# A two-layer trunk on one core: the feed forwards' norm moved into x, and twelve more column pairs by seven products

## The chip, the cores and the metric

The kernel runs on one core of a Trainium2 chip. The metric is the device time of one execution in microseconds (us); the median of several executions is compared. Engines are named as in the profile: PE (TensorE), DVE (VectorE), ACT (ScalarE), POOL (GpSimd) and SP (SyncE, which only issues DMAs).

## The reference

The input is one sequence of 512 tokens with 1024 channels. Everything is float32. Two layers run one after the other; every layer is a half-step feed forward, a mixing block and a second half-step feed forward.

```
def rms_norm(x, g):  return x * rsqrt(mean(x*x, -1) + 1e-6) * g
def swiglu(h, w_in, w_out):               # w_in 1024 x 5632, w_out 2816 x 1024
    gate, up = split(h @ w_in, 2, axis=-1)
    return (silu(gate) * up) @ w_out

layer 0:  x = x + 0.5 * swiglu(rms_norm(x, g), w_in, w_out)      # FFN1
          x = x + rwkv7_time_mix(rms_norm(x, mix_norm))          # a scan over 512 tokens, in chunks
          x = x + 0.5 * swiglu(rms_norm(x, g), w_in, w_out)      # FFN2
          k, v = shared_kv(x)                                    # keys and values, once
layer 1:  x = x + 0.5 * swiglu(rms_norm(x, g), w_in, w_out)      # FFN3
          x = x + diff_attention(rms_norm(x, mix_norm), k, v)
          x = x + 0.5 * swiglu(rms_norm(x, g), w_in, w_out)      # FFN4
```

## The kernel before

x stays on the chip as eight tiles of 128 channels by 512 tokens. A float32 product is three matmuls in fp32r (mm3, L200 to L202): each operand is split into a rounded part `hi` and the rest `lo`, and hi·hi, hi·lo and lo·hi are added in PSUM. A weight block comes by DMA into `wraw` (two buffers), ACT casts it into `whi` (L146), DVE subtracts it into `wlo` (L147); there are three buffers of each.

The stages follow each other in the trace: FFN1 (0 to 367 us), the time mix (367 to 790, with a scan over chunks from about 580 to 748), FFN2 (790 to 1147), keys and values (1147 to 1241.5), FFN3 (1241.5 to 1600.6), attention (1600.6 to 1776), FFN4 (1776 to the end).

A feed forward works on 22 blocks of 128 gate and 128 up columns, in eleven pairs j = 0, 2, ..., 20. Before it starts, x times the norm's gain g is split into `xgh` and `xgl` (eight tiles each, ten buffers). The factor that the norm still lacks is R, 1/rms of every token: the sum of squares goes through a matmul with ones (L272), ACT takes the root (L367 to L369) and DVE refines it (L370, L371). R is multiplied in after the products, since it is one number per token: `finish` computes g = pg·R (L399, DVE), silu (L400, ACT), u = pu·R (L401, DVE), u·g (L402, POOL) and splits the result into `act` for the product with w_out. The order of the work is pairs 0 to 8, the product with w_out over blocks 0 to 7, pairs 10 to 16, the next product with w_out, pairs 18 and 20, the last one.

A pair has one of two forms. The regular form is 96 matmuls of 512 tokens: 2 blocks, gate and up, 8 channel tiles, 3 matmuls. The form called `quads` takes the 2x2 blocks of a pair (gate and up columns by two halves of the channels, tokens in halves) and uses seven products in place of eight, by Strassen's scheme as Winograd arranged it: 7 x 2 x 4 x 3 = 168 matmuls of 256 tokens. It needs sums of weight blocks (made on DVE in `tmp` and in `wraw` itself, L464 to L473) and sums of halves of x (token_sums, L408 to L428, once for each feed forward, in the tile `tc`, in FFN1 in `BK`). A quad holds both `wraw` buffers and one `tmp` tile, and its products go to g and u by additions, with R multiplied in at L475, L477 and L480. The argument `seven` lists the pairs in this form: (4, 8, 10, 14) in FFN1, (4, 8, 10, 14, 18) in FFN2 and FFN4, none in FFN3, where keys and values hold the room that the sums of x would need. That is 14 quads.

Which instruction follows which on an engine is not the order of the code: a scheduler with a model of its own writes it out when the kernel is built. On the chip every engine then works through its list in that order, so an instruction that waits holds back everything behind it on its engine. SP's list holds the DMA issues.

In the scan, the argument LEAD is the number of steps by which the preparation of a unit (a chunk and a group of heads) runs ahead of its use.

Of the kernel before, what the change touches and what calls it, by code (L numbers as in the profile page):

```python
# [25 lines left out]
class Net:  # L26
# [358 lines left out]
    def ffn(self, xs, goff, w_in, w_out, aside=iter(()), xg=None, pgs=None, new_norm=True, dst=None, seven=(), sums_at=None):  # L385
# [4 lines left out]
        with tc.tile_pool(name=self.name("ffn"), bufs=2) as pool:  # L390
# [19 lines left out]
            def token_sums():  # L410


                hl = self.tl(*(sums_at or (pool, "tc")), (P, 4, 2, 4, H), F32R, bufs=1)
                for k in range(4):
                    g = [self.v("ffn_norm", goff + k + 4 * i) for i in range(2)]
                    y = self.tl(self.gp, "nsq", bufs=2)
                    nc.scalar.activation(y, xs[k], AF.Copy, scale=g[0])
# [1 line left out]
                    for i, x, gx, z in (
                        (0, xs[k][:, half[1]], g[0], y[:, half[0]]),  # L420
                        (1, xs[k + 4][:, half[1]], g[1], t[:, 0]),
                        (2, xs[k + 4][:, half[1]], g[1], y[:, half[1]]),
                        (3, xs[k + 4][:, half[0]], g[1], t[:, 1]),
                    ):
                        nc.vector.scalar_tensor_tensor(t[:, i], x, gx, z, ALU.mult, ALU.subtract)
# [1089 lines left out]
```

## Time and profile before

| | us |
|---|---|
| median of 3 runs | 2117.89 (2116.23 to 2120.51) |
| the profiled execution, own time | 2121.1 |
| its span | 2119.4 |
| PE busy in it | 2083.5 (98%) |
| DVE busy | 1382.8 (65%) |
| ACT busy | 884.5 (42%) |
| POOL busy | 184.2 (9%) |

The profile is of one execution, whose own time is 3.2 us above the median of the runs; 1.7 us of it lie outside the span. TensorE's mean granted clock in it was 0.996 of full speed. A timeline row gives the start of an instruction, its duration, engine, line, operation and operands, and in brackets how long the engine stood idle before it and on what. A duration is from start to end, and the ends of matmuls overlap the starts of the next, so the pace of matmuls is read from their starts. Likewise DVE and ACT begin the next instruction a little before the last has ended: two dependent instructions take their full durations, independent ones follow some 0.09 us sooner.

### The profile page before, as it was taken

What the parts mean: (1) busy time and instruction counts of PE and PEld (TensorE: products, weight loads), DVE (VectorE), ACT (ScalarE), POOL (GpSimd) and SP (SyncE); (2) the same over time, 40 slices, a digit from 0 to 9 for tenths busy, and PEclk for the clock granted to TensorE, in tenths of its full rate; (3) what the DMA queues carried; (4) which work ended last, traced back from release to release, by engine and by line L of the source; (5) the groups of instructions that cost most, each with busy time, mean ns of one, the idle gap of its engine ahead of it and who ended that gap; (6) DMA issues with size and microseconds to landing.
All of it is one profiled execution on the core that took longest, in us unless ns stands there. A gap on an engine that the chain in (4) does not pass through costs nothing.

```text
span 2119.4 us, 28879 instructions
## 1 busy us (share of the span) xinstructions
PE 2083.5 (98%) x11471; PEld 1798.4 (85%) x11471; DVE 1382.8 (65%) x2126; ACT 884.5 (42%) x1459; POOL 184.2 (9%) x226
## 2 busy tenths in 40 slices
PE   9999999999989999999999999999999999999999
PEld 7889888778889978989888988888889778989887
DVE  7857745897977767757466445445356857857563
ACT  6423324687235545323234343223235855423332
POOL 1100001000222201000000001001010210100000
PEclk9999999999999999999999999999999999999999
DMA  5232423336655542323323233333322112232332
GB/s 161 80 120 80 139 95 117 111 135 159 159 138 119 125 132 67 120 80 120 101 92 107 82 98 99 100 100 100 99 80 80 41 47 93 80 120 80 120 100 79
DMA packets 273139, 220.07 MB, mean 104 GB/s; under 512 B 85738, under 2 KB 257932, under 8 KB 273004
## 3 DMA queue, kind: packets, MB, share of 16 engines
q1 hardware_dynamic: 273004, 218.22, 33.8%
q8 instruction: 90, 1.47, 0.3%
q14 instruction: 45, 0.37, 0.1%
HBM read 193.55 MB, written 16.25 MB: 99 GB/s over the span
## 4 chain that ended last, share of the span: by engine, by line
PE 85%; DVE 8%; ACT 3%; DMA 3%; issue 1%; SPq 0%; POOL 0%; DVEq 0%; ACTq 0%; POOLq 0%
PE ps L200 26%; PE ps L201 26%; PE ps L202 25%; ACT s L1304 1%; PE ps L1082 1%; PE ps L1108 1%; DVE wlo L147 1%; PE ps L898 1%; PE ps L1064 1%; DMA g_d<-t 1%; PE ps L1070 1%; PE ps L1099 1%; PE ps L1097 0%; ACT whi L146 0%; DVE t L808 0%
## 5 line engine op out<-in xcount | busy, mean ns | idle before, releaser
L200 PE MATMUL ps<-xgh,whi 128*128 128x512 f32 (+1 forms) x1560 | 573.4, 369 | 1.5 <-ACT whi L146 1.0
L201 PE MATMUL ps<-xgl,whi 128*128 128x512 f32 (+1 forms) x1560 | 572.8, 367 | 0.5 <-DVE xgl L208 0.5
L202 PE MATMUL ps<-xgh,wlo 128*128 128x512 f32 (+1 forms) x1560 | 568.9, 368 | 0.4 <-DVE wlo L147 0.3
L146 ACT CAST whi<-wraw 128x1024 fp32r<-128x1024 f32 (+2 forms) x240 | 243.1, 1023 | 589.0 <-PE ps L201 447.7
L147 DVE TENSOR_TENSOR wlo<-wraw,whi 128x1024 fp32r<-128x1024 f32 (+2 forms) x240 | 311.9, 1303 | 59.3 <-ACT whi L146 53.5
L200 PEld LDWEIGHTS ps<-xgh,whi 128*128 128x128 f32 x1560 | 294.8, 189 | 53.0 <-ACT whi L146 3.2
L202 PEld LDWEIGHTS ps<-xgh,wlo 128*128 128x128 f32 x1560 | 294.5, 189 | 49.9 <-DVE wlo L147 1.4
L201 PEld LDWEIGHTS ps<-xgl,whi 128*128 128x128 f32 x1560 | 294.9, 189 | 49.2 <-issue 1.0
L201 PE MATMUL ps<-actl,whi 128*128 128x512 f32 x656 | 255.3, 389 | 0.0
L200 PE MATMUL ps<-acth,whi 128*128 128x512 f32 x656 | 254.9, 389 | 0.0
L202 PE MATMUL ps<-acth,wlo 128*128 128x512 f32 x656 | 254.3, 389 | 0.0
L402 POOL TENSOR_TENSOR u<-u,g 128x512 f32<-128x512 f32 x60 | 96.6, 1613 | 1409.0 <-DVE u L401 880.9
L528 DVE SCALAR_TENSOR_TENSOR x<-ps,x 128x512 f32<-128x512 f32 x88 | 60.5, 690 | 187.4 <-PE ps L202 187.4
L202 PEld LDWEIGHTS ps<-acth,wlo 128*128 128x128 f32 x656 | 123.1, 188 | 25.6
L200 PEld LDWEIGHTS ps<-acth,whi 128*128 128x128 f32 x656 | 123.1, 188 | 25.6
L201 PEld LDWEIGHTS ps<-actl,whi 128*128 128x128 f32 x656 | 123.1, 188 | 25.4
L447 ACT CAST whi<-wraw 128x1024 fp32r<-128x1024 f32 x70 | 73.5, 1050 | 130.9 <-PE ps L201 121.5
L200 PE MATMUL ps<-whi,xgh 128*128 128x256 f32 (+1 forms) x384 | 123.3, 323 | 0.2 <-DVE mx L1299 0.2
L401 DVE TENSOR_TENSOR u<-ps,R 128x512 f32<-128x512 f32 x60 | 41.3, 688 | 125.5 <-PE ps L202 125.5
L201 PE MATMUL ps<-wlo,xgh 128*128 128x256 f32 (+1 forms) x384 | 122.5, 319 | 0.6 <-DVE wlo L182 0.6
L202 PE MATMUL ps<-whi,xgl 128*128 128x256 f32 (+1 forms) x384 | 122.2, 318 | 0.0
L448 DVE TENSOR_TENSOR wlo<-wraw,whi 128x1024 fp32r<-128x1024 f32 x70 | 94.3, 1347 | 17.7 <-ACT whi L447 17.1
(393 smaller groups left out, 3268.1 us busy)
## 6 DMA issues: line engine op xcount, KB each, us to landing
wraw<-in_ffn_w_in_dram SPq DMA_DIRECT2D x87, 1024.0 KB
wraw<-in_ffn_w_out_dram SPq DMA_DIRECT2D x34, 1024.0 KB
wraw<-in_rwkv_w_rkv_dram SPq DMA_DIRECT2D x12, 1024.0 KB
wraw<-in_ffn_w_out_dram SPq DMA_DIRECT2D x12, 768.0 KB
wraw<-in_w_kv_dram SPq DMA_DIRECT2D x8, 1024.0 KB
am_d<-nsq SPq DMA_DIRECT2D x16, 256.0 KB
AM<-am_d SPq DMA_DIRECT2D x16, 256.0 KB
wraw<-in_diff_w_q_dram SPq DMA_DIRECT2D x4, 1024.0 KB
```

Source lines behind the costliest of these rows:

```text
L146: self.nc.scalar.copy(hi[:, ks], raw[:, :, c : c + P])
L147: (eng or self.nc.vector).tensor_sub(lo[:, ks], raw[:, :, c : c + P], hi[:, ks].bitcast(F32))
L200: mm(ps, wh, xh, start=start, stop=False)
L201: mm(ps, wh, xl, start=False, stop=False)
L202: mm(ps, wl, xh, start=False, stop=stop)
L401: nc.vector.tensor_mul(u, pu, self.R)
L402: nc.gpsimd.tensor_mul(u, u, g)
L447: nc.scalar.copy(hi, w)
L448: nc.vector.tensor_sub(lo, w, hi.bitcast(F32))
L528: nc.vector.scalar_tensor_tensor(x, ps, 0.5, x, ALU.mult, ALU.add)
L898: mm(ps[:, c, :], abd[:, c0 + c, :], BK[:, p, c0 + c, :], start=True, stop=True)
L1064: mm(pw[:, p, 0:L], Mo[:, p, :], DT[:, p, :].rearrange("p (h t) -> p h t", h=2)[:, :, 32:], start=True, stop=True)
```

## The change

For the blocks of pair 0 all stays as it was, but that u·g is now on DVE. After pair 0's products a new function `normed` computes y = x·g·R for the eight tiles (L422), splits y into new `xgh` and `xgl` (L207, L208) and makes the sums of halves from y by plain subtractions (L429 to L434). From pair 2 on the products come out with the norm in them: `finish` takes silu straight from PSUM (L405) and multiplies (L406), and the quads lose their three multiplications by R.

The lists `seven` grow to (6, 8, 10, 12, 14) in FFN1 and (6, 8, 10, 12, 14, 16, 18) in FFN2, FFN3 and FFN4: 26 quads. Now quads follow one another without a regular pair between them: 6 and 8, then 10, 12, 14 and (but for FFN1) 16. For FFN3 to have room for its sums, keys and values go out to DRAM before it (four DMAs of 1 MB issued by POOL) and come back before attention (four by SP). LEAD goes from 4 to 5.

```diff
             def finish(j, pg, pu):
                 if j % 2 == 0:
                     gu[:] = [self.tl(pool, n, (P, 2, T), bufs=1) for n in ("g", "u")]
                 g, u = (t[:, j % 2] for t in gu)
-                nc.vector.tensor_mul(g, pg, self.R)
-                nc.scalar.activation(g, g, AF.Silu)
-                nc.vector.tensor_mul(u, pu, self.R)
-                nc.gpsimd.tensor_mul(u, u, g)
+                if j < 2:
+                    nc.vector.tensor_mul(g, pg, self.R)
+                    nc.scalar.activation(g, g, AF.Silu)
+                    nc.vector.tensor_mul(u, pu, self.R)
+                    nc.vector.tensor_mul(u, u, g)
+                else:
+                    nc.scalar.activation(g, pg, AF.Silu)
+                    nc.vector.tensor_mul(u, pu, g)
                 acts[j] = self.split(pool, u, "act", 12)
...
-            def token_sums():
+            def normed():
                 hl = self.tl(*(sums_at or (pool, "tc")), (P, 4, 2, 4, H), F32R, bufs=1)
+                ys, new = {}, {}
+                for k in range(KT):
+                    y = ys[k] = self.tl(pool, "actl" if k // 4 else "acth", bufs=12)
+                    nc.vector.scalar_tensor_tensor(y, xs[k], self.v("ffn_norm", goff + k), self.R, ALU.mult, ALU.mult)
+                    new[k] = self.split(self.gp, y, "xg", XB)
+                xg[:] = [new[k] for k in range(KT)]
                 for k in range(4):
...
+                    b = [[ys[k + 4 * i][:, half[c]] for c in range(2)] for i in range(2)]
+                    sub = nc.vector.tensor_sub
+                    sub(t[:, 0], b[0][1], b[0][0])
...
                     nc.scalar.copy(hl[:, k, 0], t)
...
             def quads(j):
-                mul(g, g, self.R.unsqueeze(1).to_broadcast([P, 2, T]))
                 nc.scalar.activation(g, g, AF.Silu)
-                mul(c22, c22, R[1])
                 mul(c22, c22, c12)
                 add(c21, c21, prod(split(a22), tsum(3)))
-                mul(c21, c21, R[0])
                 mul(c21, c21, c11)
...
                     if new_norm:
                         self.R = self.rstd(xs, NORM_EPS)
-                    if seven:
-                        token_sums()
+                    normed()
                     for c in (0, 1):
                         finish(c, pg[c], pu[c])
...
-        NCH, L, G, LEAD = 8, 64, 4, 4
+        NCH, L, G, LEAD = 8, 64, 4, 5
...
-    net.ffn(xs, 0, w_in, ffn_w_out[0, 0], prepare(), xg, pgs, seven=(4, 8, 10, 14), sums_at=(net.bkp, "BK"))
+    net.ffn(xs, 0, w_in, ffn_w_out[0, 0], prepare(), xg, pgs, seven=(6, 8, 10, 12, 14), sums_at=(net.bkp, "BK"))
...
-    net.ffn(xs, KT, ffn_w_in[0, 1], ffn_w_out[0, 1], seven=(4, 8, 10, 14, 18))
+    net.ffn(xs, KT, ffn_w_in[0, 1], ffn_w_out[0, 1], seven=(6, 8, 10, 12, 14, 16, 18))
...
         net.shared_kv(xs, w_kv, kT, vN, gk)
-        net.ffn(xs, 2 * KT, ffn_w_in[1, 0], ffn_w_out[1, 0], new_norm=False)
+        for t, t_d in zip(flat, (kd, vd)):
+            for h in range(2):
+                tc.nc.gpsimd.dma_start(t_d[:, h], t[:, h])
+    net.ffn(xs, 2 * KT, ffn_w_in[1, 0], ffn_w_out[1, 0], new_norm=False, seven=(6, 8, 10, 12, 14, 16, 18))
+        kT, vN, flat = keys_values(kvq)
+        for t, t_d in zip(flat, (kd, vd)):
+            for h in range(2):
+                tc.nc.sync.dma_start(t[:, h], t_d[:, h])
         net.attention(
...
-    net.ffn(xs, 3 * KT, ffn_w_in[1, 1], ffn_w_out[1, 1], dst=out[0], seven=(4, 8, 10, 14, 18))
+    net.ffn(xs, 3 * KT, ffn_w_in[1, 1], ffn_w_out[1, 1], dst=out[0], seven=(6, 8, 10, 12, 14, 16, 18))
```

How the lists of the engines change is shown at three places. Numbers behind a name tell its buffers apart; `ps` is a PSUM tile.

PE at the end of FFN2's pair 0, before the change. ps_7060 and ps_7061 are pair 0's last two results, xgh and xgl are x·g; L272 is the matmul with ones that R hangs on.

```order
L201 MATMUL ps_7061<-xgl_7007,whi_7054 128x512
L200 MATMUL ps_7060<-xgh_7034,whi_7050 128x512
L201 MATMUL ps_7060<-xgl_7035,whi_7050 128x512
L202 MATMUL ps_7060<-xgh_7034,wlo_7051 128x512
L272 MATMUL ps_7181<-nacc_7158,ones 128x512
L202 MATMUL ps_7061<-xgh_7006,wlo_7055 128x512
L200 MATMUL ps_7061<-xgh_7010,whi_7054 128x512
```

22 more matmuls of pair 0 stand behind L272, and the next pair's behind them without a new operand.

The same place in the change. ps_7164 is the last result of pair 0; ps_7409, ps_7410 and ps_7467 belong to pair 2; xgh_7297 and xgl_7298 are the first tile of the new x·g·R.

```order
L202 MATMUL ps_7164<-xgh_7133,wlo_7158 128x512
L200 MATMUL ps_7164<-xgh_7137,whi_7157 128x512
L201 MATMUL ps_7164<-xgl_7138,whi_7157 128x512
L202 MATMUL ps_7164<-xgh_7137,wlo_7158 128x512
L272 MATMUL ps_7284<-nacc_7261,ones 128x512
L200 MATMUL ps_7409<-xgh_7297,whi_7391 128x512
L200 MATMUL ps_7410<-xgh_7297,whi_7401 128x512
L200 MATMUL ps_7467<-xgh_7297,whi_7395 128x512
L201 MATMUL ps_7409<-xgl_7298,whi_7391 128x512
L202 MATMUL ps_7409<-xgh_7297,wlo_7392 128x512
```

L272 has moved behind the last product of pair 0, and right behind it stand products of pair 2 that read the new tiles.

DVE at that place, before: L370 and L371 finish R; L399 and L401 are pair 0's multiplications by R; wlo_7259 is of a later weight block.

```order
L370 TENSOR_TENSOR nr_t_7185<-nr_t_7185,nr_a_7184 128x512
L425 SCALAR_TENSOR_TENSOR tmp_7221<-x_1022_6753,vec_103,tmp_7221 128x256
L371 SCALAR_TENSOR_TENSOR R_7183<-nr_t_7185,R_7183 128x512
L425 SCALAR_TENSOR_TENSOR tmp_7221<-x_1022_6753,vec_103,tmp_7221 128x256
L399 TENSOR_TENSOR g_7228<-ps_7058,R_7183 128x512
L401 TENSOR_TENSOR u_7229<-ps_7060,R_7183 128x512
L399 TENSOR_TENSOR g_7228<-ps_7059,R_7183 128x512
L401 TENSOR_TENSOR u_7229<-ps_7061,R_7183 128x512
L147 TENSOR_TENSOR wlo_7259<-wraw_7256,whi_7258 128x1024
L427 TENSOR_TENSOR tc_7191<-tmp_7221,tc_7191 128x1024
```

Nothing here makes an operand of pair 2's first products.

DVE at that place in the change: L422 makes y, in tiles that go by the names acth and actl; L400 and L402 are pair 0's multiplications by R; L429 is the first of the sums; L208 makes the new xgl.

```order
L422 SCALAR_TENSOR_TENSOR actl_7319<-x_1051_6855,vec_103,R_7286 128x512
L422 SCALAR_TENSOR_TENSOR actl_7325<-x_1051_6855,vec_103,R_7286 128x512
L422 SCALAR_TENSOR_TENSOR actl_7331<-x_1052_6856,vec_103,R_7286 128x512
L422 SCALAR_TENSOR_TENSOR actl_7337<-x_1052_6856,vec_103,R_7286 128x512
L400 TENSOR_TENSOR g_7371<-ps_7161,R_7286 128x512
L402 TENSOR_TENSOR u_7372<-ps_7163,R_7286 128x512
L400 TENSOR_TENSOR g_7371<-ps_7162,R_7286 128x512
L402 TENSOR_TENSOR u_7372<-ps_7164,R_7286 128x512
L429 TENSOR_TENSOR tmp_7343<-acth_7295 128x256
L208 TENSOR_TENSOR xgl_7298<-acth_7295,xgh_7297 128x512
L208 TENSOR_TENSOR xgl_7304<-acth_7301,xgh_7303 128x512
L208 TENSOR_TENSOR xgl_7310<-acth_7307,xgh_7309 128x512
```

Between R and the first xgl that pair 2 reads stand eight L422, four multiplications and a subtraction.

DVE at the end of FFN2's quad 10, before, where a regular pair follows: L448 and L469 to L480 belong to the quad; L147 are the next pair's weights.

```order
L448 TENSOR_TENSOR wlo_8439<-wraw_8243,whi_8438 128x1024
L471 TENSOR_TENSOR u_8248<-u_8248,ps_8376 128x2x256
L472 TENSOR_TENSOR u_8248<-u_8248,ps_8284 128x2x256
L477 TENSOR_TENSOR u_8248<-u_8248,R_7183 128x2x256
L147 TENSOR_TENSOR wlo_8481<-wraw_8478,whi_8480 128x1024
L474 TENSOR_TENSOR g_8247<-g_8247,ps_8408 128x2x256
L147 TENSOR_TENSOR wlo_8485<-wraw_8478,whi_8484 128x1024
L475 TENSOR_TENSOR g_8247<-g_8247,R_7183 128x1024
L479 TENSOR_TENSOR u_8248<-u_8248,ps_8442 128x2x256
L147 TENSOR_TENSOR wlo_8491<-wraw_8488,whi_8490 128x1024
L480 TENSOR_TENSOR u_8248<-u_8248,R_7183 128x2x256
L478 TENSOR_TENSOR u_8248<-u_8248,g_8247 128x2x256
```

The regular pair's weights are split among the quad's last additions and multiplications.

DVE at the end of FFN2's quad 10 in the change, where quad 12 follows: u_8377 and g_8376 belong to quad 10, L470 is quad 12's first sum of weights, and the L454 are its first two splits; L483 adds the last product of quad 10.

```order
L478 TENSOR_TENSOR u_8377<-u_8377,ps_8413 128x2x256
L454 TENSOR_TENSOR wlo_8612<-wraw_8604,whi_8611 128x1024
L480 TENSOR_TENSOR g_8376<-g_8376,ps_8537 128x2x256
L470 TENSOR_TENSOR tmp_8608<-wraw_8605 128x1024
L483 TENSOR_TENSOR u_8377<-u_8377,ps_8569 128x2x256
L482 TENSOR_TENSOR u_8377<-u_8377,g_8376 128x2x256
L476 TENSOR_TENSOR wraw_8605<-wraw_8604,wraw_8605 128x1024
L484 TENSOR_TENSOR u_8377<-u_8377,g_8376 128x2x256
L454 TENSOR_TENSOR wlo_8643<-tmp_8608,whi_8642 128x1024
L208 TENSOR_TENSOR actl_8597<-u_8377,acth_8596 128x512
```

Quad 12's second split (wlo_8643) now stands behind L483, which needs quad 10's last product, and behind three more.

## Rows read from the trace of the kernel before

**Rows 1.** The page: busy time by engine; the chain that ended last, by engine.

```profile
PE 2083.5 (98%) x11471; PEld 1798.4 (85%) x11471; DVE 1382.8 (65%) x2126; ACT 884.5 (42%) x1459; POOL 184.2 (9%) x226
...
PE 85%; DVE 8%; ACT 3%; DMA 3%; issue 1%; SPq 0%; POOL 0%; DVEq 0%; ACTq 0%; POOLq 0%
```

**Rows 2.** Windows: stretch, its us, busy of each engine, PEclk, DMA share, GB/s.

```profile
859.19:880.98 21.79, 21.79 (x98) 18.03 (x97) 17.69 (x20) 8.01 (x10) 2.11 (x1) 1.00 0.30 97
944.68:964.83 20.15, 20.15 (x169) 20.14 (x168) 14.47 (x16) 7.74 (x8) 0.00 (x0) 1.00 0.34 106
56.06:77.69 21.63, 21.03 (x170) 20.39 (x169) 18.28 (x21) 9.10 (x10) 2.14 (x1) 1.00 0.31 98
1803.96:1824.61 20.65, 20.41 (x169) 20.20 (x168) 17.56 (x20) 8.79 (x10) 1.29 (x1) 1.00 0.31 101
```

**Rows 3.** PE's timeline where FFN2's pair 2 goes over into quad 4.

```profile
880.75 0.39 PE L202 MATMUL ps<-xgh,wlo 128*128 128x512 f32 x1
880.98 0.28 PE L200 MATMUL ps<-xgh,whi 128*128 128x256 f32 x1
881.10 0.28 PE L201 MATMUL ps<-xgl,whi 128*128 128x256 f32 x1
```

**Rows 4.** PE's timeline in the scan, at two waits.

```profile
615.84 0.49 PE L1129 MATMUL ps<-xgl,bd 128*128 128x512 f32 x1
620.78 1.38 PE L1064 MATMUL ps<-whi,wlo 128*128 128x64 f32 x8 [4.44 <-DMA whi<-inv_d]
...
726.98 1.25 PE L1108 MATMUL ps<-KM,Vb 128*128 128x128 f32 x5 [1.24 <-DVE KM L1101]
```

**Rows 5.** Windows behind those two waits, columns as in rows 2.

```profile
622.00:624.00 2.00, 2.00 (x11) 2.00 (x11) 1.74 (x6) 0.30 (x1) 0.93 (x3) 0.50 0.09 12
...
727.00:731.00 4.00, 4.00 (x20) 3.79 (x21) 2.84 (x10) 2.62 (x9) 1.49 (x4) 0.57 0.91 220
```

**Rows 6.** Timelines of PE, ACT and DVE where FFN2's R is made.

```profile
811.39 1.02 PE L272 MATMUL ps<-nacc,ones 128*128 128x512 f32 x2
...
813.26 0.68 ACT L367 ACTIVATE R<-ps,bias 128x512 f32<-128x512 f32 x1
...
814.41 0.62 ACT L369 ACTIVATE nr_t<-R 128x512 f32<-128x512 f32 x1
...
818.22 0.68 DVE L401 TENSOR_TENSOR u<-ps,R 128x512 f32<-128x512 f32 x1
818.82 0.68 DVE L399 TENSOR_TENSOR g<-ps,R 128x512 f32<-128x512 f32 x1
```

**Rows 7.** The instructions of line 727, x·g·R in the time mix (duration in ns).

```profile
L727 DVE SCALAR_TENSOR_TENSOR h<-x,vec,R x8: 742/744/746, 383.7 to 388.4; 128x512 f32<-128x512 f32 x8
```

**Rows 8.** ACT's timeline before FFN1's R, and at the end of keys and values.

```profile
29.96 1.28 ACT L367 ACT_TABLE_LOAD   x1
...
1239.71 2.73 ACT L1229 ACTIVATE vN<-ps,Rn 128x512 f32<-128x512 f32 x4 [1.96 <-PE ps L202]
```

**Rows 9.** Timelines of SP and ACT at the end of FFN2's quad 10; a DMA issue; attention.

```profile
956.09 2.95 SPq L135 DMA_DIRECT2D wraw<-in_ffn_w_in_dram  x2
...
961.35 2.00 ACT L146 CAST whi<-wraw 128x1024 fp32r<-128x1024 f32 x2 [3.97 <-DMA wraw<-in_ffn_w_in_dram]
...
1631.62 1.13 PE L1298 MATMUL ps<-kT,qT 64*128 64x512 f32 x4
```

**Rows 10.** DVE's timeline at the end of FFN2's quad 10.

```profile
963.57 0.68 DVE L474 TENSOR_TENSOR g<-g,ps 128x512 f32<-128x512 f32 x1
...
965.31 1.22 DVE L475 TENSOR_TENSOR g<-g,R 128x1024 f32<-128x1024 f32 x1
966.44 0.68 DVE L479 TENSOR_TENSOR u<-u,ps 128x512 f32<-128x512 f32 x1
```

**Rows 11.** ACT's cast of a weight block in quads, by line.

```profile
L447 ACT CAST whi<-wraw 128x1024 fp32r<-128x1024 f32 x70 | 73.5, 1050 | 130.9 <-PE ps L201 121.5
```

**Rows 12.** The chain, a DMA that writes 256 KB to DRAM.

```profile
415.21 6.25 DMA g_d<-t
```

More of the change, by code (lines that the diff above doesn't have):

```diff
@@ L408, in ffn @@
             half = (slice(0, H), slice(H, T))
-            def token_sums():
+            def normed():
                 hl = self.tl(*(sums_at or (pool, "tc")), (P, 4, 2, 4, H), F32R, bufs=1)
+                ys, new = {}, {}
[4 more added lines that the diff above has]
+                xg[:] = [new[k] for k in range(KT)]
                 for k in range(4):
-                    g = [self.v("ffn_norm", goff + k + 4 * i) for i in range(2)]
-                    y = self.tl(self.gp, "nsq", bufs=2)
-                    nc.scalar.activation(y, xs[k], AF.Copy, scale=g[0])
+                    b = [[ys[k + 4 * i][:, half[c]] for c in range(2)] for i in range(2)]
                     t = self.tl(pool, "tmp", (P, 4, H), bufs=1)
[L419 to L425, printed above, removed]
+                    sub = nc.vector.tensor_sub
+                    sub(t[:, 0], b[0][1], b[0][0])
+                    sub(t[:, 1], b[1][1], t[:, 0])
+                    sub(t[:, 2], b[1][1], b[0][1])
+                    sub(t[:, 3], b[1][0], t[:, 1])
                     nc.scalar.copy(hl[:, k, 0], t)
-                    nc.vector.tensor_sub(hl[:, k, 1], t, hl[:, k, 0].bitcast(F32))
+                    sub(hl[:, k, 1], t, hl[:, k, 0].bitcast(F32))
                 sums.append(hl)
@@ L441, in quads @@
                 g, u = (self.tl(pool, n, (P, 2, T), bufs=1) for n in ("g", "u"))
-                R = [self.R[:, h].unsqueeze(1).to_broadcast([P, 2, H]) for h in half]
                 def split(w):
@@ L1471, in trunk, with keys_values @@
     net.early.close()
-    net.ffn(xs, KT, ffn_w_in[0, 1], ffn_w_out[0, 1], seven=(4, 8, 10, 14, 18))
+    net.ffn(xs, KT, ffn_w_in[0, 1], ffn_w_out[0, 1], seven=(6, 8, 10, 12, 14, 16, 18))
+    drm = ctx.enter_context(tc.tile_pool(name="kvd", bufs=1, space=bass.MemoryType.DRAM))
+    kd, vd = (drm.tile([P, 2, 4 * T], F32, name=n) for n in ("k_d", "v_d"))
+    def keys_values(pool):
+        kT, vN = net.tl(pool, "kT", (P, KT, T)), net.tl(pool, "vN", (P, 4, C))
+        flat = [t.rearrange("p a b -> p (a b)").rearrange("p (h n) -> p h n", h=2) for t in (kT, vN)]
+        return kT, [vN[:, t] for t in range(4)], flat
     with tc.tile_pool(name="kvp", bufs=1) as kvp:
-        kT = net.tl(kvp, "kT", (P, KT, T))
-        vN = [net.tl(kvp, f"vN{t}", (P, C)) for t in range(4)]
+        kT, vN, flat = keys_values(kvp)
         gk = kvp.tile([P, P], F32, tag="gk", name="gk")[:, 0:1]
@@ L1478, in trunk @@
         net.shared_kv(xs, w_kv, kT, vN, gk)
-        net.ffn(xs, 2 * KT, ffn_w_in[1, 0], ffn_w_out[1, 0], new_norm=False)
+        for t, t_d in zip(flat, (kd, vd)):
+            for h in range(2):
+                tc.nc.gpsimd.dma_start(t_d[:, h], t[:, h])
+    net.ffn(xs, 2 * KT, ffn_w_in[1, 0], ffn_w_out[1, 0], new_norm=False, seven=(6, 8, 10, 12, 14, 16, 18))
+    with tc.tile_pool(name="kvq", bufs=1) as kvq:
+        kT, vN, flat = keys_values(kvq)
+        for t, t_d in zip(flat, (kd, vd)):
+            for h in range(2):
+                tc.nc.sync.dma_start(t[:, h], t_d[:, h])
         net.attention(
```

## The prediction

> **What bounds the kernel.** I read the page first: PE is busy for 98% of the span and makes 85% of the chain of waits that ended last; DVE is at 65%, ACT at 42% [rows 1]. Then PE's timeline and windows by stage, since those shares are means. In the feed forwards PE has practically no gap; the waits that are left lie in the scan [rows 4]. So the time is the sum of PE's matmuls at their pace plus PE's waits. An edit on DVE, ACT or POOL costs nothing as long as the operands of the next product are there, and everything from the moment they are not. What counts is therefore (a) how much PE work goes, and (b) at which places the new lists let PE run into DVE. DVE's mean hides (b): in FFN2's quad 10 it is busy for 14.5 of 20.15 us, and PE's weight loads fill 20.14 of them [rows 2].
>
> **Part 1: twelve more quads.** A regular pair takes 21.79 us, a quad 20.15 [rows 2]. That is 96 matmuls at 0.227 us against 168 at 0.120 (21.79/96, 20.15/168) [rows 2, 3]. Each pair changed saves 1.64 us, and 12 of them 19.7 us.
> The Trainium skill ("TensorE: Matmul & The Clock Gate", section "Back-to-back issue gap") gives for an isolated matmul N/2.4 + 2.5 ns, which is 215.8 ns for 512 columns and 109.2 for 256. By it, as an estimate, a pair would save 20.72 - 18.35 = 2.37 us and twelve 28.4. The rows differ: 227 and 120 ns, and the sum goes by them.
>
> **Part 2: LEAD 5, and two small waits.** In the scan PE stands for 4.44 us at 620.78 until a DMA brings inv_d [rows 4]. With LEAD 5 the list puts that first unit one step later, when the DMA has landed: -4.44. Behind the gap the clock granted is 0.50, the level of 1.2 GHz in place of 2.4 [rows 5]; I take the same shape as behind the gap of 1.24 us at 726.98, where it was 0.57 over 4 us, that is 4 x 0.43 = 1.7 us lost [rows 4, 5]. Sum -6.1; bounds -6.1 and, if LEAD 5 merely moves the wait and one more unit crowds the buffers, +2 (from -4.4 to a wait half as long again). The first quads of FFN1 and FFN4 took 21.63 and 20.65 us because their sums came late [rows 2]; now the first quad stands a pair later: -1.5 - 0.5 = -2.0.
>
> **Part 3: the seam behind pair 0.** Before, R was wanted only after the products. Now pair 2's products read x·g·R, and in FFN2 the list puts L272 behind pair 0's last product and only three hi·hi products that need xgh between it and the first that needs xgl. So PE waits for this chain, from the end T of pair 0 in FFN2: L272 1.02 and, up to the start of L367, 813.26 - 811.39 = 1.87 in the row (0.85 of it ACT's other work; I take 1.2); three ACT steps, 813.26 to 815.03 = 1.77; DVE's L370 and L371 dependent, 0.72 + 0.69: R at about T + 4.4. Then eight L422 by the analogue L727, 5.30 us from 383.7 in steps of 0.66 (its own duration is 0.744) [rows 7]; four multiplications at 0.60 (818.22 to 818.82) [rows 6]; a subtraction 0.40 (half the size; estimate) and the first xgl 0.70: T + 13.2. Off go the three matmuls, 0.68, and the 0.45 that L272 cost PE before too: FFN2 +12.1. FFN4 has the table load of 1.28 us on ACT in front of R as FFN1 has it [rows 8]: +13.4. In FFN1 L272 stands 22 matmuls (5.0 us) ahead of the end, so +8.0. In FFN3 R is known from before, and DVE can start at once if `y` finds its buffers.
> There keys and values decide: y's tiles lie where these were, so the first L422 waits for four POOL DMAs. The last of vN is written by 1239.71 + 2.73 = 1242.44, or 0.9 us into FFN3 (which starts at 1241.55) [rows 8]. No POOL DMA occurs in the trace. From one side, two weight loads of 1 MB are issued within 2.95 us of 956.09, and the first is in use at 961.35 [rows 9]: 5.3 us for one, some 8 for both; y starts 9 us in, its splits are there at 18.3, and PE wants them at the end of pair 0's gate and up, 17.2: +1.1. From the other side, 256 KB to DRAM took 6.25 us [rows 12]; were the 4 MB to go at that pace without overlap, they would take 100 us, with four in parallel 25: +17. I take +1.1, nearest to the rows of the same size, and keep 0 to 17.
> The Trainium skill ("DMA: Bandwidth & Descriptors", section "Anatomy of one DMA — SWDGE (gpsimd) path") gives 2.0 us + bytes/436e3; as an estimate 6.8 us for 2 MB. No run here shows it; the sum would stay the same, as pair 0 hides it.
> Seams: 12.1 + 13.4 + 8.0 + 1.1 = +34.6. A wait over 1.2 us is followed in the trace by half clock [rows 4, 5]: +1.7 three times, +5.1.
>
> **Part 4: quads behind quads.** Before, each quad had a regular pair or a product with w_out behind it, where DVE caught up. Now 15 quads follow a quad: three in FFN1 and four in each of the others. DVE's list at such a place (FFN2, 10 to 12) is: wlo of p1', L480, L470, L483, L482, L476, L484, wlo of p2'. L483 needs the last product of the old quad, which ends at E. So from E: 0.2 handover, L483 and L482 at 0.60, L476 1.14, L484 0.60, and wlo of p2' lasts from 3.14 to 4.36 (0.69 and 1.22 for one, steps of 0.60 and 1.13) [rows 10]. p1' gives PE 24 x 0.120 = 2.88 us, and its successor's third matmul needs that wlo at E + 3.12: wait 1.24. Then p3': its sum L472 ends at E + 6.3, ACT's cast of 1.05 [rows 11] at 7.4, wlo at 8.64, wanted at 7.3 to 7.4: another 1.25. Together 2.5 us a transition, and some 2.8 where the quad ahead was itself late and the loads of wu with it: 8 x 2.5 + 7 x 2.8 = +39.6. The consecutive quad then lasts 22.7 us, longer than the regular pair it replaces. Bounds: 0, if DVE gets ahead by more than the list shows (it is busy for 17 (1.14) + 9 to 11 x 0.6, some 19 us of 20.15), and 15 x 3.7 = 55, if both waits (each 1.25) bring the half clock of rows 5 at a third of its price. The weights themselves come in time: the next pair's loads are issued 11.4 us into a quad (956.09 - 944.68) [rows 2, 9].
>
> **Part 5: at nothing.** R's multiplications go from finish and quads, and u·g goes from POOL to DVE: PE waits for neither before, since DVE and POOL run beside it [rows 1]. The multiplications' room on DVE is in part 4's list already. Reloading keys and values: issued from 1600.6, used first at 1631.62 [rows 9], 31 us for 4 MB, at the pace of 8 us for 2 MB some 16: 0, at worst +4. SP has the w_q blocks behind them, which are prefetched. The spill beside FFN3's weight loads: the DMA share there is about 0.3 [rows 2], 0 to 2.
>
> **Sum.** -19.7 - 6.1 - 2.0 + 34.6 + 5.1 + 39.6 = +51.5, rounded to +52. 2121.1 + 52 = 2173 for an execution as the profiled one; less 3.2, since that one lay 3.2 us above the median: 2170 us.
>
> **Rivals.**
> *A. The quads' transitions are hidden.* DVE and ACT work further ahead than the list lets me see, and only the seams cost: 52 - 39.6 = +12.4, 2131 us. For it: DVE waits for ACT and PE in a quad, 5.7 us of 20.15 idle [rows 2]. Against: the order is fixed, and L483 cannot run before the old quad's end. 17%.
> *B. All waits are dearer.* Half clock behind every transition (15 x 1.1 = +16) or FFN3's spill at the slow bound (+16): 2186 to 2202 us. For it: 0.50 behind gaps of 1.24 us [rows 4, 5]. Against: the two waits of a transition are each just at that size. 14%.
> *C. Not slower.* DVE's and ACT's work is ready early at both places: R in the middle of pair 0 and the first xgl before pair 0's last product, and no transition waits. Then -19.7 - 6.1 - 2.0 = -28, 2090 us. It decides if DVE's 13 us of chain fit under pair 0, which would need L272 some 58 matmuls earlier than the list has it in FFN2. The list speaks against it. 6% with its partial forms.
> *D. The twelve quads cost as much as regular pairs.* A quad's weight loads fill PE already [rows 2], so there is no slack; this is forecast plus 0 to 10, within its range.
> By the page's pace above the sum would be 8.7 us lower, 2161; that pace is contradicted by rows 2 and gets 2%.
>
> **Chances.** The forecast (both seams and transitions wait) 61%, A 17%, B 14%, C 6%, page's pace 2%. The range 2128 to 2200 takes in A and leaves out C and the top of B, about one in ten; the forecast's own is 2150 to 2186. A measurement of this kernel tells 0.2% or 4.2 us from no change: faster 5% (C), same 3% (between C and A), slower 92%.
>
> **What the profile will show.** Right: three gaps of PE of 7 to 13 us behind L272 in FFN1, FFN2 and FFN4, released by DVE's xgl, with clock 0.5 behind them; two gaps of about 1.2 us in the second and third product of every quad that follows a quad, released by DVE's wlo (L454); a lone quad of 20.15 us; no 4.4 us gap at the start of the scan; attention's first QK product at once after its operands. Wrong: consecutive quads of 20.15 us, xgl ready before L272's result is read, a PE gap at attention's start released by the reload, or FFN3's first y later than 10 us into the stage.

## The result, and the profile after

The changed kernel takes 2185.1 us (2184.23 to 2185.68, 4 runs) against 2119.2 for the kernel before in the same runs: a ratio of 1.031, 95% interval 1.0294 to 1.0326. Forecast were 2170 us and slower. Page of the changed kernel, the parts that answer to [rows 1]:

```profile
PE 2088.6 (96%) x12335; PEld 1837.9 (84%) x12335; DVE 1475.7 (68%) x2292; ACT 935.6 (43%) x1519; POOL 89.9 (4%) x170
...
PE 73%; DVE 15%; DMA 5%; ACT 4%; issue 2%; SPq 0%; POOL 0%; ACTq 0%; DVEq 0%
```

PE's share of the chain falls from 85% to 73%, DVE's doubles: PE now runs into DVE. Stage by stage (from the starts of the stages' first products in the two timelines), of the 63.4 us that the span grew; FFN4's pair 0 begins at about 1760 before and ends at 1782.2, so FFN4 starts earlier than the 1776 given in the section on the kernel before:

| stretch | before | after | difference |
|---|---|---|---|
| FFN1 | 367.3 | 384.7 | +17.4 |
| time mix, and FFN2 to the end of pair 0 | 450.0 | 448.4 | -1.6 |
| FFN2, the rest | 329.4 | 352.4 | +23.0 |
| keys and values | 94.9 | 94.9 | 0 |
| FFN3 | 359.0 | 360.0 | +1.0 |
| attention, and FFN4 to the end of pair 0 | 181.6 | 179.9 | -1.7 |
| FFN4, the rest, and the end | 337.2 | 362.5 | +25.3 |

The list of what PE waited for (us in total, times, longest) has two causes at its head, DVE's wlo and the new tiles of x, for which PE waited no more than 0.5 us in the kernel before:

```profile
PE ps L202 <- DVE wlo L454: 24.5, 15, 2.4
PE ps L201 <- DVE xgl L208: 17.4, 4, 5.7
PE ps L200 <- ACT xgh L207: 11.4, 3, 6.1
```

**The seam behind pair 0**, FFN2: PE's timeline, then DVE's.

```profile
833.07 1.02 PE L272 MATMUL ps<-nacc,ones 128*128 128x512 f32 x2
838.85 1.65 PE L200 MATMUL ps<-xgh,whi 128*128 128x512 f32 x3 [4.76 <-ACT xgh L207]
846.17 0.80 PE L201 MATMUL ps<-xgl,whi 128*128 128x512 f32 x1 [5.67 <-DVE xgl L208]
```

```profile
836.67 0.69 DVE L371 SCALAR_TENSOR_TENSOR R<-nr_t,R 128x512 f32<-128x512 f32 x1
837.39 2.74 DVE L422 SCALAR_TENSOR_TENSOR acth<-x,vec,R 128x512 f32<-128x512 f32 x4
840.05 2.73 DVE L422 SCALAR_TENSOR_TENSOR actl<-x,vec,R 128x512 f32<-128x512 f32 x4
842.70 0.68 DVE L400 TENSOR_TENSOR g<-ps,R 128x512 f32<-128x512 f32 x1
...
845.42 1.89 DVE L208 TENSOR_TENSOR xgl<-acth,xgh 128x512 fp32r<-128x512 f32 x3
```

R is done 4.3 us behind the end of pair 0 (833.07), the first xgl at 13.1 us, where PE goes on: the prediction had 4.4 and 13.2 [rows 6, 7]. Windows (columns as in rows 2) of PE's restart and of FFN2's quads 10, 12 and 14, and the lone quad 18:

```profile
846.00:850.00 4.00, 3.83 (x9) 3.07 (x10) 4.00 (x9) 0.00 (x0) 0.00 (x0) 0.50 0.00 0
...
977.53:997.69 20.16, 20.16 (x170) 20.15 (x169) 13.05 (x14) 6.77 (x7) 0.00 (x0) 1.00 0.33 106
997.69:1021.73 24.04, 21.89 (x171) 21.68 (x170) 20.51 (x24) 10.88 (x12) 0.00 (x0) 0.93 0.28 88
1021.73:1044.65 22.92, 20.92 (x171) 20.37 (x170) 20.05 (x24) 9.82 (x11) 0.00 (x0) 1.00 0.29 92
1110.91:1131.06 20.15, 20.15 (x169) 20.15 (x168) 13.87 (x15) 8.34 (x9) 0.00 (x0) 1.00 0.33 105
```

The clock granted behind the seam is 0.50, as in [rows 5]. A lone quad takes 20.15 us as in [rows 2]; one behind another 22.6 to 24.6 over the kernel, more than the regular pair it replaced (21.79). **A transition**, 6 to 8 in FFN2 (the old quad ends at 911.19), on DVE and then on PE:

```profile
911.68 0.68 DVE L483 TENSOR_TENSOR u<-u,ps 128x512 f32<-128x512 f32 x1
912.28 0.69 DVE L482 TENSOR_TENSOR u<-u,g 128x512 f32<-128x512 f32 x1
912.88 1.22 DVE L476 TENSOR_TENSOR wraw<-wraw,wraw 128x1024 f32<-128x1024 f32 x1
914.02 0.69 DVE L484 TENSOR_TENSOR u<-u,g 128x512 f32<-128x512 f32 x1
914.62 1.22 DVE L454 TENSOR_TENSOR wlo<-tmp,whi 128x1024 fp32r<-128x1024 f32 x1
```

```profile
915.89 0.39 PE L202 MATMUL ps<-tc,wlo 128*128 128x256 f32 x1 [1.42 <-DVE wlo L454]
919.66 0.39 PE L200 MATMUL ps<-xgh,whi 128*128 128x256 f32 x1 [0.44 <-ACT whi L453]
```

Between the old quad's last addition and the second wlo stand three operations that PE does not need then. The wait before the third product, which the prediction put at 1.25 us, is only 0.44 us: two matmuls of the fourth product (on xgh and xgl) stand ahead of the one that wants that wlo. Eleven transitions cost 2.4 to 2.8 us each, four cost 3.9 to 4.4: 10 to 12, the first of its run, in FFN1 to FFN3, where the first wait is 2.2 to 2.4 us, and 14 to 16 in FFN4, with 0.8 and 1.8 us. The clock falls behind these (mean 0.93 over quad 12, above). In FFN3 the first L422 stands 7.7 us into the stage (9 forecast) and waits for POOL's last store of 1 MB, issued 6.5 us before (1281.54):

```profile
1288.02 2.74 DVE L422 SCALAR_TENSOR_TENSOR acth<-x,vec,R 128x512 f32<-128x512 f32 x4 [4.58 <-DMA v_d<-vN]
```

The Trainium skill ("DMA: Bandwidth & Descriptors", section "Anatomy of one DMA — SWDGE (gpsimd) path") would give, as an estimate, 4.4 us for 1 MB; another store of 1 MB was issued 1.4 us ahead of this one (1280.18), so the row speaks neither for that figure nor against it.

### The profile page after: what moved, and what is told of

It reads as the page before. It is cut to its first block, busy times and chain, and to the rows that moved or that the text cites. A ratio compares the mean times of both kernels' runs of the same rounds, so it can differ in the third digit from the quotient of the medians.

```text
span 2182.8 us, 30783 instructions
## 1 busy us (share of the span) xinstructions
PE 2088.6 (96%) x12335; PEld 1837.9 (84%) x12335; DVE 1475.7 (68%) x2292; ACT 935.6 (43%) x1519; POOL 89.9 (4%) x170
## 4 chain that ended last, share of the span: by engine, by line
PE 73%; DVE 15%; DMA 5%; ACT 4%; issue 2%; SPq 0%; POOL 0%; ACTq 0%; DVEq 0%
PE ps L202 22%; PE ps L200 22%; PE ps L201 22%; DMA wraw<-in_ffn_w_in_dram 4%; DVE wlo L454 2%; ACT whi L453 1%; ACT s L1306 1%; DVE wraw L476 1%; PE ps L900 1%; DVE wlo L147 1%; DVE x L937 1%; PE ps L1084 1%; PE ps L1110 0%; DVE xmt L754 0%; DVE u L483 0%
## 5 line engine op out<-in xcount | busy, mean ns | idle before, releaser
L200 PE MATMUL ps<-xgh,whi 128*128 128x512 f32 (+1 forms) x1464 | 510.6, 351 | 18.6 <-ACT xgh L207 11.4
L201 PE MATMUL ps<-xgl,whi 128*128 128x512 f32 (+1 forms) x1464 | 508.6, 348 | 17.4 <-DVE xgl L208 17.4
L202 PE MATMUL ps<-xgh,wlo 128*128 128x512 f32 (+1 forms) x1464 | 505.8, 348 | 0.5 <-DVE wlo L147 0.3
L201 PEld LDWEIGHTS ps<-xgl,whi 128*128 128x128 f32 x1464 | 280.4, 192 | 53.6 <-DVE xgl L208 19.7
L147 DVE TENSOR_TENSOR wlo<-wraw,whi 128x1024 fp32r<-128x1024 f32 (+2 forms) x192 | 226.1, 1184 | 108.7 <-ACT whi L146 97.1
L453 ACT CAST whi<-wraw 128x1024 fp32r<-128x1024 f32 x130 | 135.3, 1049 | 247.4 <-PE ps L201 151.6
L202 PE MATMUL ps<-tc,wlo 128*128 128x256 f32 x672 | 194.4, 289 | 19.3 <-DVE wlo L454 19.3
L200 PE MATMUL ps<-tc,whi 128*128 128x256 f32 x672 | 193.2, 288 | 0.8 <-ACT whi L453 0.8
L201 PE MATMUL ps<-tc,whi 128*128 128x256 f32 x672 | 192.1, 286 | 0.0
L454 DVE TENSOR_TENSOR wlo<-wraw,whi 128x1024 fp32r<-128x1024 f32 x130 | 158.1, 1223 | 48.0 <-ACT whi L453 47.6
L202 PEld LDWEIGHTS ps<-tc,wlo 128*128 128x128 f32 x672 | 131.0, 195 | 21.9 <-DVE wlo L454 21.7
L202 PEld LDWEIGHTS ps<-acth,wlo 128*128 128x128 f32 x656 | 123.2, 188 | 25.6
L200 PEld LDWEIGHTS ps<-tc,whi 128*128 128x128 f32 x672 | 131.0, 195 | 2.4 <-ACT whi L453 1.2
```

The source lines that it names most:

```text
L147: (eng or self.nc.vector).tensor_sub(lo[:, ks], raw[:, :, c : c + P], hi[:, ks].bitcast(F32))
L200: mm(ps, wh, xh, start=start, stop=False)
L201: mm(ps, wh, xl, start=False, stop=False)
L202: mm(ps, wl, xh, start=False, stop=stop)
L453: nc.scalar.copy(hi, w)
L454: nc.vector.tensor_sub(lo, w, hi.bitcast(F32))
```

## Experiments

Edits are to the changed kernel. Ratios are to the kernel before, with 95% intervals. "Transitions" are what runs of quads last beyond 20.15 us each, summed over the kernel from PE's timeline; in the changed kernel that is 46.0 us for 15. Matmuls of the next product that stand among a quad's are not counted to it.

**1. R behind the products again** (finish, token_sums, quads of before).

```diff
-                    normed()
+                    if seven:
+                        token_sums()
```

> The changed kernel with R multiplied after the products again (finish, quads and token_sums as before); lists, LEAD 5 and the spill stay. Theory: the seams behind pair 0 cost 40 us (8.8 in FFN1, 14.4 in FFN2, 0.3 in FFN3, 16.4 in FFN4), so all four go; at a transition DVE's list now has wlo of the second product some 1.3 us sooner, so a transition costs 1.2 to 2.5 us instead of 3.1. Sum 2122 to 2147, point 2135 us. Rival (the gaps behind pair 0 come from the longer lists, which crowd the weight buffers, and not from x): gaps of 10 us stay at pair 0, 2165 us or more.

2161.2 us, 1.0187 (1.0171 to 1.0203). The seams are gone, so they came from x and not from the lists; but the saving is 24 us, not 40 or more, since the transitions grew to 60.4 us (I had expected them to shrink). DVE's window of one such quad (and 0.4 us of the next) points at the reason: with R's multiplications it is busy for 22.46 of 23.98 us. In span the saving is 2182.8 - 2157.1 = 25.7 us; 40.0 of seams less 14.4 of dearer transitions make 25.6.

```profile
976.52:1000.50 23.98, 21.41 (x172) 20.58 (x170) 22.46 (x26) 10.61 (x12) 0.00 (x0) 1.00 0.27 88
```

**2. No quad behind another.**

```diff
-seven=(6, 8, 10, 12, 14)        # FFN1
+seven=(6, 10, 14)
-seven=(6, 8, 10, 12, 14, 16, 18)
+seven=(6, 10, 14, 18)
```

> The changed kernel with seven = (6, 10, 14) in FFN1 and (6, 10, 14, 18) in the others: 15 quads, none behind another. Theory: the 15 transitions cost 46 us, so they go, and 11 pairs fewer by seven products give 11 x 1.64 = 18 us back: 2157 us (2152 to 2162), every quad 20.15 us. Rival (a quad costs more in this kernel wherever it stands, since the loads of its two buffers come late): quads of 21 to 23 us, 2185 us or more.

2156.91 us, 1.0171 (1.0154 to 1.0188): as expected. All 15 quads take 20.15 us (one 20.24); adjacency costs 46 us, a quad by itself nothing.

**3. Three operations of a transition on POOL.**

```diff
-                nc.vector.tensor_sub(a21, a11, a21)
+                (nc.gpsimd if j - 2 in seven else nc.vector).tensor_sub(a21, a11, a21)
...
+                late = nc.gpsimd.tensor_mul if j + 2 in seven and j != 8 else mul
-                mul(c22, c22, c12)
+                late(c22, c22, c12)
```

> The changed kernel with three operations of a transition on POOL instead of DVE: the last two multiplications of a quad that another follows, and the subtraction for the fifth product of a quad that follows another. Theory (DVE's order makes the second and third product of the next quad late): wlo of the second product now ends some 2.0 to 2.5 us behind the old quad's end and is wanted at 3.1, so 35 to 46 of the 46 us go: 2139 to 2150. Rival (the weights' loads are late, since a quad holds both buffers until its end): the gaps move but stay, at most 10 us go, 2175 us or more.

2206.55 us, 1.0398 (1.0377 to 1.0418): a miss, transitions 68 us. DVE's and POOL's timelines at 6 to 8:

```profile
919.56 1.23 DVE L454 TENSOR_TENSOR wlo<-tmp,whi 128x1024 fp32r<-128x1024 f32 x1 [0.60 <-ACT whi L453]
920.82 3.31 DVE L472 TENSOR_TENSOR tmp<-tmp,wraw 128x1024 f32<-128x1024 f32 x1
```

```profile
918.34 1.30 POOL L483 TENSOR_TENSOR u<-u,g 128x512 f32<-128x512 f32 x1 [137.50 <-ACT g L481]
919.59 3.45 POOL L476 TENSOR_TENSOR wraw<-wraw,wraw 128x1024 f32<-128x1024 f32 x1
923.01 2.24 POOL L485 TENSOR_TENSOR u<-u,g 128x512 f32<-128x512 f32 x1
```

L472 takes 1.22 us elsewhere and 3.31 beside POOL's L476; it ends 1.1 us after that one, and POOL's L485 takes 2.24 in place of the 1.30 of L483. The two engines take turns on operations with two inputs in SBUF, so the work was not taken off DVE. The Trainium skill says so ("SBUF — State Buffer", section "Terms": the port pair that the two engines share is held for the full instruction and the loser blocks); this trace agrees. The run decides nothing between order and loads.

**4. The norm into x behind pair 2**, whose products go channel tile by channel tile like pair 0's.

```diff
-                if j == 0:
+                if j < 4:
...
-                    normed()
+                    if j == 2:
+                        normed()
                     for c in (0, 1):
-                        finish(c, pg[c], pu[c])
+                        finish(j + c, pg[c], pu[c])
```

> The changed kernel with the norm going into x behind pair 2 instead of pair 0; pair 2 runs its products channel tile by channel tile like pair 0, so that old tiles come free one by one, and its results get R behind the products. Theory (the seam is the chain from L272 to the first new xgl, 13 us, with nothing for PE to do): pair 2's 21.8 us hide it, 36 to 41 of the 40 us of seams go, 2144 to 2149. Rival (it is not the chain but DVE's and ACT's whole work on the new tiles, 26 us and more with the sums, that PE waits for sooner or later): half of it comes back in front of pair 4 or quad 6, 2160 to 2170.

2159.75 us, 1.0177 (1.0159 to 1.0194): 25 us, at the lower edge of the rival. Between pair 0 and the first quad PE's gaps are 0.15 us in FFN2 and 1.76 in FFN4, none in the others: the chain is hidden. But in FFN1, FFN2 and FFN4 the first two quads together now last some 4 us longer (12 in all): DVE works on the sums until the first one begins, as the rival had it. PE's timeline there, FFN2:

```profile
881.16 0.39 PE L200 MATMUL ps<-tc,whi 128*128 128x256 f32 x1 [1.68 <-ACT whi L453]
882.42 0.39 PE L202 MATMUL ps<-tc,wlo 128*128 128x256 f32 x1 [0.76 <-DVE wlo L454]
```

**5. LEAD 4.** One number (LEAD = 4).

> The changed kernel with LEAD 4 again. Theory (the 4.4 us that LEAD 5 takes out at the start of the scan come back some 40 us later, as waits for operands that pass through DRAM, since the scan goes at the pace of these): the gap of about 4.4 us is there again, the later waits go, the scan ends within 1 us of where it did, 2184 to 2187 us. Rival, the prediction's term: +6.1, 2191 us.

2186.84 us, 1.0308 (1.0294 to 1.0322): as expected, LEAD is worth nothing. PE's waits in the scan, first in this kernel, then in the changed one:

```profile
635.50 1.94 PE L1066 MATMUL ps<-whi,wlo 128*128 128x64 f32 x8 [4.21 <-DMA whi<-inv_d]
```

```profile
642.15 1.13 PE L1084 MATMUL ps<-AM,whi 128*128 128x128 f32 x8 [1.28 <-DVE whi L1080]
...
663.02 2.05 PE L1084 MATMUL ps<-AM,whi 128*128 128x128 f32 x8 [2.34 <-DVE wraw L1167]
```

Without the first wait [rows 4] PE is some 7 us further ahead; within the next 30 us it stands at other operands, and from its first product to its last the scan is 0.5 us shorter than before (0.7 with LEAD 4). In the run with quads apart that later wait is one of 3.5 us for AM, which goes through DRAM. What sets the scan's pace was not tried.

**6. DVE's order at the transitions by hand.**

`end` holds the close of a quad: its last addition, two multiplications and the splits.

```diff
-                    nc.vector.tensor_sub(lo, w, hi.bitcast(F32))
+                    self.lo = nc.vector.tensor_sub(lo, w, hi.bitcast(F32))
...
-                add(c21, c11, prod(split(s1), tsum(1)))
...
+                p3 = prod(split(s1), tsum(1))
+                with tc.issue_after(self.lo.ins):
+                    nc.vector.tensor_sub(a21, a11, a21)
+                p4 = prod(split(a12), raw(4, 0))
+                with tc.issue_after(self.lo.ins):
+                    while ends:
+                        ends.pop()()
...
+                ends.append(end)
+                if j == 8 or j + 2 not in seven:
+                    ends.pop()()
```

> The changed kernel with another order on DVE at the transitions and nothing else: the close of a quad (its last addition, two multiplications, the splits) stands behind the split for the next quad's fourth product, and the subtraction for the fifth product behind the split for the third. Theory (the order, not the amount of DVE work or the loads): first gap gone, second short, as the chain of six operations from the sum to the third wlo is 6.6 us long and starts just before the old quad's end: 0.3 to 1.3 us a transition instead of 3.1; 2145 to 2160, point 2152 us. Rival A (amount: DVE has 19 us of work in 20.15): the waits move to the fourth to seventh product, over 2170 us. Rival B (loads: both buffers are held until the quad's end): gaps before the first and second product, 2165 us or more.

2188.94 us, 1.0322 (1.0307 to 1.0338): a miss; my theory as it stood falls. The two waits at the transition are gone from 6 to 8 (0.7 us left), but the next weights are late: the first load for the product with w_out is issued 5.9 us before quad 8 ends (922.22 and 928.1), in the changed kernel 8.2 us (925.81 and 933.99), and is in use 6.9 us after its issue. ACT waits for it, then PE:

```profile
929.14 1.99 ACT L146 CAST whi<-wraw 128x1024 fp32r<-128x1024 f32 x2 [5.74 <-DMA wraw<-in_ffn_w_out_dram]
```

```profile
930.24 0.50 PE L200 MATMUL ps<-acth,whi 128*128 128x512 f32 x1 [1.98 <-ACT whi L146]
```

In the runs from 10 to 16 the waits just move. The order is one part of the cause; rival B, the loads, is the other, as experiments 9 and 10 show.

**7. Norm behind pair 2, no quad behind another, the first at 8** (experiment 4 with seven = (8, 10, 14, 18), FFN1 (8, 10, 14)).

> The norm behind pair 2 (as in the run before) and no quad behind another, the first at 8, so that the sums have a pair more: seven = (8, 10, 14, 18), FFN1 (8, 10, 14), 15 quads. Theory: nothing of seams (40) and transitions (46) is left but the matmul with ones, and 11 pairs cost 18 us more than by seven products: 2185 - 40 - 46 + 18 = 2117, with 2 to 4 us of small waits 2117 to 2121 us, no different from before. Rival (the sums' 4 us waits of the run before were DVE's overload by the new tiles): they come back in front of quad 8, 2129 to 2133.

2120.15 us, 1.0001 (0.9992 to 1.001). As expected: seams and transitions account for what the change costs, to within the 2 to 4 us of small waits, and with a pair more the sums are in time.

**8. Experiments 4 and 6 together, the first quad at 8** (seven = (8, 10, 12, 14, 16, 18), FFN1 (8, 10, 12, 14)).

> The norm behind pair 2, DVE's other order at the transitions, and the first quad at 8: seven = (8, 10, 12, 14, 16, 18), FFN1 (8, 10, 12, 14), 22 quads, 11 transitions (three from 10 to 16, two in FFN1). Theory: before 2119, eight quads more -13, LEAD and first quads -2, transitions 11 x 0.3 to 1.3 = 3 to 14: 2107 to 2118, point 2112 us, faster than before by 0.3%. Rival: transitions still cost 2 us or more, so that a quad behind a quad gains nothing over a regular pair: 2119 to 2130.

2148.37 us, 1.0133 (1.0115 to 1.015): a miss, dearer than the rival too. Eleven transitions still cost 39.6 us. With two buffers the order is no cure.

**9. A third weight buffer for the quads**, nothing ordered by hand.

```diff
-                wg, wu = (self.tl(self.wp, "wraw", (P, 8, 256), bufs=2) for _ in range(2))
+                wg, wu = (self.tl(p, n, (P, 8, 256), bufs=b) for p, n, b in ((pool, "wx", 1), (self.wp, "wraw", 2)))
...
-                acts[j] = self.split(pool, u, "act", 12)
+                acts[j] = self.split(pool, u, "act", 10)
```

> The changed kernel with a third buffer of weights for the quads: wg has one of its own and wu takes turns in the two old ones, so that the next quad's wu is there early; act has 10 buffers instead of 12 to make room. Nothing is ordered by hand; with the load early the scheduler itself puts the second split ahead of the old quad's close. Theory (loads and order together: while both buffers are held, the loop of load, sum, two splits and release has no slack at 20.15 us, so an order alone could only move the wait): nearly all of the 46 us of transitions go, 0 to 0.5 us left of each, 2139 to 2148. Rival (DVE's amount of work, 19 of 20.15 us, is what a run of quads cannot hold): over 2165 us, with waits in the middle of the quads.

2151.45 us, 1.0155 (1.014 to 1.017): 34 us less than the change, transitions 12.1 us instead of 46.0. The pairs 6 and 8 last 40.31 us together. DVE's timeline there: the second wlo stands ahead of L483 now, since its sum was made earlier. So the buffer changed the order too, without an edit to it.

```profile
901.74 1.22 DVE L454 TENSOR_TENSOR wlo<-tmp,whi 128x1024 fp32r<-128x1024 f32 x1
903.02 0.69 DVE L483 TENSOR_TENSOR u<-u,ps 128x512 f32<-128x512 f32 x1
903.62 0.68 DVE L482 TENSOR_TENSOR u<-u,g 128x512 f32<-128x512 f32 x1
```

**10. Third buffer and order by hand** (experiments 6 and 9).

> The third weight buffer and the order by hand at the transitions (the close of a quad behind the next one's fourth split). Theory (loads and order together): as with the third buffer alone, 2139 to 2150 us, since either order fits once the loads are early; the hand-made order alone had cost 2189. Rival (amount of DVE work): over 2165 us.

2141.31 us, 1.01 (1.0083 to 1.0117): transitions 2.4 us. With early loads the hand-made order saves another 10 us; with late ones it saved none.

**11. All cures** (experiments 4, 6 and 9; seven as in 8).

> All three cures together: the norm into x behind pair 2, the third weight buffer with the order by hand at the transitions, and the first quad at 8, seven = (8, 10, 12, 14) in FFN1 and (8, 10, 12, 14, 16, 18) in the others, 22 quads. Theory: nothing of seams and transitions is left but 0.3 us each; from before: eight quads more -13, small waits of the first quads -2, LEAD -1, matmuls with ones 0: 2119 - 16 + 3 = 2106 us (2102 to 2112). Rival (the cures get in each other's way on DVE, as the sums did with the norm behind pair 2): 2115 to 2125.

2112.68 us, 0.9969 (0.9957 to 0.998): faster than the kernel before by 0.3%, though 6.7 us above the 2106 expected and just outside the 2102 to 2112; where these 6.7 us are was not followed up. Windows of quads 12 and 14 of FFN2:

```profile
966.20:986.40 20.20, 20.20 (x170) 20.20 (x170) 18.68 (x23) 9.33 (x12) 0.00 (x0) 1.00 0.32 104
986.40:1006.60 20.20, 20.20 (x171) 20.20 (x169) 18.84 (x22) 8.94 (x11) 0.00 (x0) 1.00 0.30 99
```

DVE is busy for 18.7 to 18.8 of 20.2 us and PE does not wait: the amount of its work was not the cause.

**12. Pair 20 by seven products as well** (FFN2 to FFN4, 25 quads).

> The same with pair 20 by seven products too in FFN2 to FFN4, 25 quads. Theory: three more quads save 4.9 us, and the close of the last quad stands before the last product with w_out, which needs its two blocks 2.7 us after it begins, while the close takes some 3: 1 us each. Against the other kernel of this call -2 (-5 to +1): 2104 us. Rival (nothing hides the close there): +3.

2110.16 us, 0.9955 (0.9942 to 0.9968): the fastest of all here; 2.5 us less than the kernel above, as expected of the difference, with ranges that overlap only just (2106.82 to 2110.93 and 2109.56 to 2114.43).

## Why the prediction was right, and where its sizes were off

The direction and the two causes were right: the lists of before and after show what PE would have to wait for, and the trace of before has the durations. Term by term:

| term | forecast | measured in the two profiles |
|---|---|---|
| twelve more quads | -19.7 | -19.7 (21.79 and 20.15 us as before) |
| LEAD 5 | -6.1 | -0.5 |
| first quads | -2.0 | -1.9 |
| seams, with the clock | +39.7 | 8.9, 14.4, 0.3 and 16.4 in FFN1 to FFN4 (the stage's difference less its other terms): +40.0 |
| transitions | +39.6 | +46.0 |
| rest | 0 | about -0.5: +2.0 in FFN1's first 16 us, where the profiles of the other kernels here lie between -0.8 and +2.8 of before, and small gains elsewhere, among them twice the 0.45 us of L272, which the forecast had taken off the seams |
| sum | +51.5 | +63.4 |

That the seams' sum comes out so close is partly luck: by itself FFN1's was forecast 0.8 us too high (8.0 and 1.7 for the clock), FFN3's 0.8 too high, FFN2's 0.6 and FFN4's 1.3 too low. The chain itself was right: in FFN2 13.1 us against 13.2.

The step that failed is part 2, "-6.1; bounds -6.1 and ... +2": I took a wait on a path that ends elsewhere as if PE set the scan's pace. The wait went and others came (experiment 5); the term belonged nearer its other bound.

The second, smaller: the 39.6 for the transitions, which measured 46.0. Most of the 6.4 us lies in the four dear ones, with 3.9 to 4.4 us each, where the bound "both waits bring the half clock at a third of its price" had 3.7. In each of them one of the next quad's two loads is late. In FFN2 it is wg: quad 12's was issued 11.4 us into quad 10 as forecast (988.94 - 977.53), but its first cast is at 994.95, 6.0 us later, where the row of before had 5.3 [rows 9]. The trace names PE as what ended that wait of ACT; but from 6 to 8 the same cast stands 16.7 us into the quad, against 17.4 here, and waits for the load:

```profile
907.73 1.05 ACT L453 CAST whi<-wraw 128x1024 fp32r<-128x1024 f32 x1 [3.99 <-DMA wraw<-in_ffn_w_in_dram]
...
994.95 1.05 ACT L453 CAST whi<-wraw 128x1024 fp32r<-128x1024 f32 x1 [4.72 <-PE ps L201]
```

In the other three it is wu, in use 6.7 to 7.4 us after its issue, and DVE's sum L470 waits 1.2 to 1.3 us for it. FFN1's:

```profile
196.88 1.23 DVE L470 TENSOR_TENSOR tmp<-wraw 128x1024 f32<-128x1024 f32 x1 [1.23 <-DMA wraw<-in_ffn_w_in_dram]
```

I wrote that "the weights themselves come in time", from the 11.4 us of a lone quad. That holds for the first transition of a run at most. Behind it the issue slips: wg of quad 14 in FFN2 is issued 1013.37 - 997.69 = 15.7 us into quad 12.

```profile
1013.37 0.37 SPq L445 DMA_DIRECT2D wraw<-in_ffn_w_in_dram  x1
```

Experiments 6, 9 and 10 show that these loads and DVE's order act together. That the loop of load, sum, split and release has no slack at 20.15 us with two buffers is my reading of this; no run shows it by itself.

Two smaller slips in the working changed little. "A wait over 1.2 us is followed in the trace by half clock" was read from two rows; the trace of before has a longer wait with the full clock behind it, and the changed kernel's waits of 1.4 us have it too (last section). And "17 (1.14) + 9 to 11 x 0.6, some 19 us" does not add up as written; a quad behind a quad has 11 of the long operations and 11 of the short, 11 x 1.14 + 11 x 0.6 = 19.1, and the windows show 18.7 to 20.5 us.

Rival A (transitions hidden) was refuted by every transition; B was right in kind for the clock in those four; C had no sign. R's multiplications cost nothing in the kernel before, as said, but between quads that follow one another they would: experiment 1, where they are back, has 14.4 us more of transitions. The reload of keys and values costs nothing: no wait of PE for it stands in the list.

## What to carry to other kernels

Price a new dependence by the whole list ahead of its producer, in the order in which the engine will run it: seven operations too many and four that could have waited made 13 us out of a chain of about 6 (an estimate from the rows: R at 4.3 us, then one L422, one cast and one subtraction of 0.6 to 0.7 each). Where two dense stages come to stand behind each other, ask what the gap between them did before: here it hid the loads and the close. Try an engine's order and its buffers together: of 46 us the order alone saved nothing, the third buffer alone 34 (the list then changed by itself), both 44. And to remove a wait off the path that sets the pace is no gain.

## What the runs showed of the hardware

Not expected: an operation with both inputs in SBUF took 3.31 us on DVE instead of 1.22 beside one on POOL (experiment 3), while L484, one of whose inputs is in PSUM, keeps its 0.68. So moving such work from DVE to POOL freed DVE of nothing here.

The clock behind a gap of PE does not go by the gap's length alone. In the changed kernel a gap of 1.42 us (at 915.89) left it at 1.00, one of 2.15 us was followed by 0.60:

```profile
916.00:920.00 4.00, 3.56 (x26) 3.21 (x27) 3.49 (x5) 2.75 (x4) 0.00 (x0) 1.00 0.00 0
...
1003.12 0.39 PE L202 MATMUL ps<-tc,wlo 128*128 128x256 f32 x1 [2.15 <-DVE wlo L454]
...
1003.12:1007.00 3.88, 3.88 (x21) 3.88 (x22) 3.37 (x4) 2.46 (x3) 0.00 (x0) 0.60 0.00 0
```

In the scan of the kernel before, a gap of 1.73 us left it at 1.00, where that of 1.24 us was followed by 0.57 [rows 4, 5]:

```profile
581.21 1.08 PE L1064 MATMUL ps<-whi,wlo 128*128 128x64 f32 x8 [1.73 <-DMA whi<-inv_d]
...
580.00:584.00 4.00, 2.02 (x16) 1.86 (x16) 3.78 (x11) 0.37 (x1) 0.00 (x0) 1.00 0.33 51
```

What decides it was not tried.
